# Low parts and two-operand arithmetic from GpSimd to VectorE in a two-layer hybrid diffusion block

## The chip, the cores and the metric

The kernel runs on one core of one Trainium2 chip. A core has five instruction queues that matter here: TensorE (PE in the profile; its weight loads are listed apart, as PEld), VectorE (DVE), ScalarE (ACT), GpSimd (POOL) and SyncE (SP), which issues most DMAs. The metric is the device time of one execution in microseconds; less is better.

## The reference

A backbone of two layers (`DEPTH` = 2) over 256 latent tokens and 256 context tokens of 1024 features. Each layer is:

```
xn = rmsnorm(x) * (1 + scale) + shift            # scale, shift from silu(c) @ w_mod
u  = xn @ w_in                                   # one projection for all three mixers
ya = latent attention, yb = windowed attention with sinks, yc = gated DeltaNet, both directions
y  = (ga*(ya @ w_pa) + gb*(yb @ w_pb) + gc*(yc @ w_pc)) @ w_out
x  = x + gate * y
x  = x + gate * ((silu(a) * b) @ w_down),   a, b = split(dwconv(xn2 @ w_up))
```

Context tokens go through the same weights; in the last layer only what the latent tokens need of them is computed. Inside the DeltaNet, per chunk of 64 tokens and per head:

```
decay = exp(min(gam[i] - gam[j], 0))
a     = strict_lower(k_beta k^T * decay);  qk = lower(q k^T * decay)
u, w  = triangular_solve(a + I, [v*beta, k*beta*exp(gam)])
scan over chunks: v_new = u - w S;  o = q S + qk v_new;  S = S*exp(g_last) + k^T v_new
```

All inputs and outputs are float32. After the two layers a last norm gives the output (1, 256, 1024).

## The kernel before

**Matrix products.** Each float32 operand is taken apart into a high part (rounded to `fp32r`, the type in which TensorE reads it) and a low part (operand minus high part). A product is then three matmuls that add up in one PSUM tile, `mm3` (lines 203 to 206): weight high by activation high (L204), weight high by activation low (L205), weight low by activation high (L206). Two helpers make the parts:

- `load_split` (L186 to 196) loads a piece of weights (`raw`, mostly 128x1024), lets ScalarE cast it to the high part (`wh`, L194) and calls `split_L` (L184) for the low part `wl = raw - wh`.
- `split` (L198 to 200) does the same for activations: cast on ScalarE (L199), difference on VectorE (L200).

`split_L` chooses the engine for `wl` by an accumulator: a fraction `lpool` of the calls goes to GpSimd, the rest to VectorE. The fraction is set per stage: 1.0 for the first modulation, 0 for the projections and the DeltaNet, 0.33 from the attention on and in the feed-forward network (FFN).

**Other work of GpSimd.** GpSimd also does elementwise steps with two SBUF operands: the running sum of squares of a norm (L372); in the DeltaNet's decay `gdn_decay` the gate by a triangle (L809), the decay by the lower mask (L822), beta by a constant (L830) and their product (L834); the scaling by beta in the solve (L921); the state's decay and an addition in the scan (L964, L991); the output norm (L1015); steps of the rotary embedding (L1182, L1237, L1257, L1258, and a copy at L1270); the sum of the merged branches (L1547); and the FFN's product `silu(a) * b` (L1627), whose result goes straight into `split`. Besides, it takes small powers for norms (L348), memsets, masks, some one-operand normalizations of the attention and a few DMAs.

**Stages.** A set-up with the first modulation; per layer the projections and gates, in whose matmuls the DeltaNet's decay, solve and scan are woven (the projections fill TensorE while the DeltaNet's chain waits); attention; merge and `w_out`; and the FFN, two halves of 11 blocks of 128 features, each an up projection and then a down projection. The FFN of the first layer works on 512 columns, that of the last on 256.

**Order.** The instruction streams are fixed when the program is built: a scheduler puts each engine's instructions in order by dependences and priorities (the program can raise the priority of one instruction; such instructions go through a wrapper at L131, so the profile shows them as L131), and each engine then works its queue strictly in that order. In the DeltaNet, `gdn_decay` makes `N` out of the exponential `d`, the products with the keys (`times_k`, L131) and L834; `N` is transposed on VectorE (STREAM_TRANSPOSE, L131), and the solve's matmuls (L845) or the scan's (L957, L971) come in between.

## Time and profile before

| | us |
| --- | --- |
| runs | 1787.89, 1794.27, 1797.77 (median 1794.27) |
| profiled execution: its own time | 1803.63 |
| its span | 1801.8 |
| TensorE busy / idle in the span | 1689.5 / 112.3 |
| VectorE, ScalarE, GpSimd busy | 1082.6, 767.2, 456.0 |

The mean granted TensorE clock of this execution was 0.962. The stages by the timeline: set-up and modulation 0 to 45 us, first projection to 84, DeltaNet of layer 0 with projections to 410, attention to 540, merge and `w_out` to 720, FFN to about 1120; for the last layer projections and DeltaNet to 1410, attention to 1500, merge to 1575, FFN and last norm to the end.

How to read it: busy times are sums over the span, and stages differ much in what they ask of VectorE and GpSimd, so windows of 45 us say more than the sums. A wait is given as "line <- engine and line that ended it". In the timeline a row is one instruction, or several of one line that follow one another (x2, x4), with the engine's wait before it in brackets.

### The profile page before, as it was taken

How to read it: one execution, taken by the hardware profiler on the slowest of the kernel's cores; microseconds unless marked ns; L12 is line 12 of the kernel's file. 1: busy time of each engine (PE TensorE's matmuls, PEld its weight loads, DVE VectorE, ACT ScalarE, POOL GpSimd, SP SyncE). 2: the span in 40 equal slices, each digit the busy share in tenths (PEclk: the TensorE clock that was granted, in tenths of full speed). 3: DMA queues.
4: the chain of work that ended last, by engine and by line, in shares of the span. 5: the costliest groups of instructions: out<-in, count | busy, mean ns of one | idle time of the engine just before them, and what ended most of it. 6: DMA issues, size and time to landing. Idle time of an engine off the chain costs nothing. (4 is left out here: it accounts for less than half of the span.)

```text
span 1801.8 us, 31553 instructions
## 1 busy us (share of the span) xinstructions
PE 1689.5 (94%) x12723; PEld 1371.2 (76%) x12723; DVE 1082.6 (60%) x2089; ACT 767.2 (43%) x1371; POOL 456.0 (25%) x351
## 2 busy tenths in 40 slices
PE   7989888999999999999999999989889899999997
PEld 4768766776557888668888888768777668989996
DVE  2896594565775433445334434798886866466573
ACT  3644411234665233334324333565433564554453
...
GB/s 341 114 80 108 96 88 164 68 85 101 45 117 155 184 136 109 311 170 94 97 103 93 94 155 155 94 88 131 100 100 30 81 59 138 239 122 169 182 171 111
DMA packets 216944, 228.75 MB, mean 127 GB/s; under 512 B 51228, under 2 KB 195422, under 8 KB 215646
## 3 DMA queue, kind: packets, MB, share of 16 engines
...
q8 instruction: 100, 1.64, 0.4%
q14 instruction: 46, 0.38, 0.1%
...
## 5 line engine op out<-in xcount | busy, mean ns | idle before, releaser
L194 ACT CAST wh<-raw 128x1024 fp32r<-128x1024 f32 (+2 forms) x294 | 298.4, 1016 | 412.8 <-PE mm L205 212.8
L184 DVE TENSOR_TENSOR wl<-raw,wh 128x1024 fp32r<-128x1024 f32 (+1 forms) x224 | 280.3, 1252 | 201.9 <-ACT wh L194 182.3
L204 PE MATMUL mm<-xnh,wh 128*128 128x512 f32 (+2 forms) x1072 | 381.6, 357 | 5.6 <-ACT wh L194 2.4
L206 PE MATMUL mm<-xnh,wl 128*128 128x512 f32 (+2 forms) x1072 | 376.1, 353 | 2.6 <-DVE wl L184 1.3
L205 PE MATMUL mm<-xnl,wh 128*128 128x512 f32 (+2 forms) x1072 | 375.5, 351 | 0.7 <-DVE xnl L411 0.6
L184 POOL TENSOR_TENSOR wl<-raw,wh 128x1024 fp32r<-128x1024 f32 (+2 forms) x70 | 162.5, 2322 | 448.7 <-ACT wh L194 419.2
L204 PEld LDWEIGHTS mm<-xnh,wh 128*128 128x128 f32 (+1 forms) x1072 | 206.4, 193 | 39.6 <-issue 7.6
L206 PEld LDWEIGHTS mm<-xnh,wl 128*128 128x128 f32 (+1 forms) x1072 | 205.7, 192 | 33.1 <-issue 2.9
L205 PEld LDWEIGHTS mm<-xnl,wh 128*128 128x128 f32 (+1 forms) x1072 | 206.4, 193 | 28.1 <-DVE xnl L411 2.2
L204 PE MATMUL g<-xnh,wh 128*128 128x256 f32 (+1 forms) x496 | 167.9, 340 | 1.4 <-ACT xnh L410 1.4
L206 PE MATMUL g<-xnh,wl 128*128 128x256 f32 (+1 forms) x496 | 166.6, 337 | 2.1 <-POOL wl L184 2.1
L205 PE MATMUL g<-xnl,wh 128*128 128x256 f32 (+1 forms) x496 | 166.3, 337 | 0.2 <-DVE xnl L411 0.2
L204 PE MATMUL mm<-s,wh 128*128 128x256 f32 (+1 forms) x458 | 151.0, 331 | 2.3 <-ACT s L199 1.7
L206 PE MATMUL mm<-s,wl 128*128 128x256 f32 (+1 forms) x458 | 150.8, 330 | 1.7 <-POOL wl L184 1.1
L205 PE MATMUL mm<-s,wh 128*128 128x256 f32 (+1 forms) x458 | 150.5, 329 | 0.1
L204 PEld LDWEIGHTS g<-xnh,wh 128*128 128x128 f32 x496 | 94.7, 192 | 15.4 <-issue 3.7
L205 PE MATMUL g<-s,wh 128*128 128x512 f32 (+1 forms) x304 | 103.6, 341 | 2.4 <-DVE s L200 2.4
L204 PE MATMUL g<-s,wh 128*128 128x512 f32 (+1 forms) x304 | 104.1, 342 | 1.3 <-ACT s L199 1.3
L206 PEld LDWEIGHTS g<-xnh,wl 128*128 128x128 f32 x496 | 94.6, 191 | 13.2 <-POOL wl L184 2.9
L206 PE MATMUL g<-s,wl 128*128 128x512 f32 (+1 forms) x304 | 103.3, 340 | 0.0
L205 PEld LDWEIGHTS g<-xnl,wh 128*128 128x128 f32 x496 | 94.8, 192 | 10.0 <-DVE xnl L411 0.8
L1627 POOL TENSOR_TENSOR b<-b,b 128x512 f32<-128x512 f32 (+1 forms) x44 | 54.6, 1240 | 170.9 <-DVE b L1611 149.6
...
## 6 DMA issues: line engine op xcount, KB each, us to landing
...
```

The costliest lines, as they stand in the source:

```text
L184: e.tensor_tensor(out=out, in0=x, in1=h.bitcast(F32), op=ALU.subtract)
L194: nc.scalar.copy(H, raw)
L204: mm(ps, lhsT=wH, rhs=xH, start=start, stop=False)
L205: mm(ps, lhsT=wH, rhs=xL, start=False, stop=False)
L206: mm(ps, lhsT=wL, rhs=xH, start=False, stop=stop)
L1627: nc.gpsimd.tensor_tensor(out=y[:, cs], in0=y[:, cs], in1=av[t][:, cs], op=ALU.mult)
```

## The change

`split_L` loses the accumulator and always uses VectorE. Every GpSimd instruction named above that has two operands, and the copy at L1270, is issued on VectorE in its place. The stage fractions (`lpool`, `lp0`, `lpg`, `lpn`, `lpb`) go away. GpSimd keeps the powers of L348, the memsets, the masks, the one-operand normalizations and its DMAs. What is computed stays the same. The queue of GpSimd goes from 294 instructions to 39, that of VectorE from 1981 rows to 2262 (a row can stand for several instructions). The lines shift by 5 to 15: L184 is L179 in the new kernel, L200 L195, L809 L803, L815 L809, L822 L816, L825 L819, L834 L828, L961 L955, L1378 L1372, L1609 and L1611 L1598 and L1600, L1627 L1616.

```diff
@@ -176,12 +176,7 @@
-        self.lacc += self.lpool
-        e = self.nc.vector
-        if self.lacc >= 1.0:
-            self.lacc -= 1.0
-            e = self.nc.gpsimd
-        e.tensor_tensor(out=out, in0=x, in1=h.bitcast(F32), op=ALU.subtract)
+        self.nc.vector.tensor_tensor(out=out, in0=x, in1=h.bitcast(F32), op=ALU.subtract)
...
@@ -369,7 +364,7 @@
-        (e or nc.gpsimd).tensor_tensor(out=self.acc[:, cs], in0=self.acc[:, cs], in1=sq[:, cs], op=ALU.add)
+        (e or nc.vector).tensor_tensor(out=self.acc[:, cs], in0=self.acc[:, cs], in1=sq[:, cs], op=ALU.add)
...
@@ -806,7 +800,7 @@
-                nc.gpsimd.tensor_tensor(out=rg[:, ph], in0=gt["g"][:, s, ph, tl, :].unsqueeze(2).to_broadcast([128, 8, 64]),
+                nc.vector.tensor_tensor(out=rg[:, ph], in0=gt["g"][:, s, ph, tl, :].unsqueeze(2).to_broadcast([128, 8, 64]),
...
@@ -819,7 +813,7 @@
-                    nc.gpsimd.tensor_tensor(out=qk[:, tl, ph], in0=Eq[:, ph],
+                    nc.vector.tensor_tensor(out=qk[:, tl, ph], in0=Eq[:, ph],
...
@@ -827,11 +821,11 @@
-                nc.gpsimd.tensor_tensor(out=bm[:, ph], in0=gt["be"][:, s, ph, tl, :].unsqueeze(2).to_broadcast([128, 8, 64]),
+                nc.vector.tensor_tensor(out=bm[:, ph], in0=gt["be"][:, s, ph, tl, :].unsqueeze(2).to_broadcast([128, 8, 64]),
-            nc.gpsimd.tensor_tensor(out=N[:, tl], in0=d, in1=bm, op=ALU.mult)
+            nc.vector.tensor_tensor(out=N[:, tl], in0=d, in1=bm, op=ALU.mult)
...
@@ -918,7 +912,7 @@
-            nc.gpsimd.tensor_tensor(out=XT[hs, tl, ph], in0=XT[hs, tl, ph],
+            nc.vector.tensor_tensor(out=XT[hs, tl, ph], in0=XT[hs, tl, ph],
...
@@ -961,7 +955,7 @@
-                    nc.gpsimd.tensor_tensor(out=Sn, in0=St, in1=gt["egl"][:, s, ph, tl].unsqueeze(3).to_broadcast([128, 2, 4, 64]), op=ALU.mult)
+                    nc.vector.tensor_tensor(out=Sn, in0=St, in1=gt["egl"][:, s, ph, tl].unsqueeze(3).to_broadcast([128, 2, 4, 64]), op=ALU.mult)
...
@@ -1012,7 +1006,7 @@
-            nc.gpsimd.tensor_tensor(out=hd(oacc[:, tl, :]), in0=hd(oacc[:, tl, :]), in1=r[:, tl, :].unsqueeze(2).to_broadcast([128, 8, 64]), op=ALU.mult)
+            nc.vector.tensor_tensor(out=hd(oacc[:, tl, :]), in0=hd(oacc[:, tl, :]), in1=r[:, tl, :].unsqueeze(2).to_broadcast([128, 8, 64]), op=ALU.mult)
...
@@ -1234,7 +1228,7 @@
-            nc.gpsimd.tensor_tensor(out=t1, in0=xq[:, lat], in1=self.con("cmla"), op=ALU.mult)
+            nc.vector.tensor_tensor(out=t1, in0=xq[:, lat], in1=self.con("cmla"), op=ALU.mult)
...
@@ -1254,8 +1248,8 @@
-            nc.gpsimd.tensor_tensor(out=x, in0=x, in1=self.con("cswa"), op=ALU.mult)
-            nc.gpsimd.tensor_tensor(out=x, in0=x, in1=t2, op=ALU.add)
+            nc.vector.tensor_tensor(out=x, in0=x, in1=self.con("cswa"), op=ALU.mult)
+            nc.vector.tensor_tensor(out=x, in0=x, in1=t2, op=ALU.add)
...
@@ -1624,7 +1613,7 @@
-                    nc.gpsimd.tensor_tensor(out=y[:, cs], in0=y[:, cs], in1=av[t][:, cs], op=ALU.mult)
+                    nc.vector.tensor_tensor(out=y[:, cs], in0=y[:, cs], in1=av[t][:, cs], op=ALU.mult)
...
```

The lines left out are the parameters, the places that set `lpool`, and the same exchange of engine at L408 (which issues nothing with these parameters), L991, L1182, L1270 and L1547.

No priority is changed, but the scheduler places the queues anew. Three places show what that does.

**First place: the second decay of the last layer.** VectorE's queue between the decay and the scan, before. The first operand `s_1898` is `d`, `s_1880` the masked decay `qk`, `s_1879` is `N`, `s_1923` its transpose, and L961 gives the operand for which TensorE's L971 waits.

```order
L131 TENSOR_TENSOR s_1898_11316<-s_1898_11316,g_11372 128x8x64
L131 TENSOR_TENSOR s_1898_11316<-s_1898_11316,g_11382 128x8x64
L184 TENSOR_TENSOR wl_11521<-raw_11518,wh_11520 128x1024
L131 STREAM_TRANSPOSE s_1923_11505<-s_1879_11225 128x1024
L131 TENSOR_TENSOR s_1880_11226<-s_1880_11226,g_11448 128x8x64
L131 TENSOR_TENSOR s_1880_11226<-s_1880_11226,g_11458 128x8x64
L131 TENSOR_TENSOR s_1880_11226<-s_1880_11226,g_11468 128x8x64
L131 TENSOR_TENSOR s_1880_11226<-s_1880_11226,g_11478 128x8x64
L131 STREAM_TRANSPOSE s_1923_11505<-s_1879_11225 32x1024 x2
L961 TENSOR_TENSOR b_1930_11536<-g_11488,gtb_10178 128x512
```

The same place after:

```order
L179 TENSOR_TENSOR wl_11521<-raw_11518,wh_11520 128x1024
L816 TENSOR_TENSOR s_1880_11226<-s_1901_11323,cst 128x512 x2
L131 TENSOR_TENSOR s_1898_11316<-s_1898_11316,g_11372 128x8x64
L131 TENSOR_TENSOR s_1898_11316<-s_1898_11316,g_11382 128x8x64
L131 TENSOR_TENSOR s_1880_11226<-s_1880_11226,g_11448 128x8x64
L828 TENSOR_TENSOR s_1879_11225<-s_1898_11316,s_1902_11331 128x1024
L131 TENSOR_TENSOR s_1880_11226<-s_1880_11226,g_11458 128x8x64
L131 TENSOR_TENSOR s_1880_11226<-s_1880_11226,g_11468 128x8x64
L131 TENSOR_TENSOR s_1880_11226<-s_1880_11226,g_11478 128x8x64
L131 STREAM_TRANSPOSE s_1923_11505<-s_1879_11225 128x1024
L955 TENSOR_TENSOR b_1930_11536<-g_11488,gtb_10178 128x512
L131 STREAM_TRANSPOSE s_1923_11505<-s_1879_11225 32x1024 x2
```

The three products that GpSimd made (L816 twice, L828) now stand in VectorE's queue, and L961 (L955 after) is put ahead of the two transposes of 32 partitions instead of behind them.

**Second place: the second decay of layer 0.** VectorE's queue before; `s_142` and `s_282` are the two masked decays that the products with queries fill, `s_325` is the transpose of `N` (`s_281`).

```order
L131 STREAM_TRANSPOSE s_325_2121<-s_281_1854 128x1024
L131 TENSOR_TENSOR s_142_769<-s_142_769,g_2008 128x8x64
L131 TENSOR_TENSOR s_142_769<-s_142_769,g_2018 128x8x64
L131 TENSOR_TENSOR s_142_769<-s_142_769,g_2028 128x8x64
L131 TENSOR_TENSOR s_142_769<-s_142_769,g_2038 128x8x64
L131 TENSOR_TENSOR s_282_1855<-s_282_1855,g_2048 128x8x64
L131 TENSOR_TENSOR s_282_1855<-s_282_1855,g_2058 128x8x64
L131 TENSOR_TENSOR s_282_1855<-s_282_1855,g_2068 128x8x64
L131 TENSOR_TENSOR s_282_1855<-s_282_1855,g_2078 128x8x64
L131 STREAM_TRANSPOSE s_325_2121<-s_281_1854 32x1024 x2
L961 TENSOR_TENSOR b_327_2150<-g_2089,gtb_754 128x512
```

After:

```order
L131 TENSOR_TENSOR s_142_769<-s_142_769,g_2028 128x8x64
L131 TENSOR_TENSOR s_142_769<-s_142_769,g_2038 128x8x64
L131 TENSOR_TENSOR s_282_1855<-s_282_1855,g_2048 128x8x64
L131 TENSOR_TENSOR s_282_1855<-s_282_1855,g_2058 128x8x64
L131 TENSOR_TENSOR s_282_1855<-s_282_1855,g_2068 128x8x64
L131 TENSOR_TENSOR s_282_1855<-s_282_1855,g_2078 128x8x64
L131 TENSOR_TENSOR s_297_1927<-s_297_1927,g_1963 128x8x64
L131 TENSOR_TENSOR s_297_1927<-s_297_1927,g_1973 128x8x64
L955 TENSOR_TENSOR b_327_2150<-g_2089,gtb_754 128x512
L828 TENSOR_TENSOR s_281_1854<-s_297_1927,s_301_1942 128x1024
L179 TENSOR_TENSOR wl_2236<-raw_2233,wh_2235 128x1024
L131 STREAM_TRANSPOSE s_325_2121<-s_281_1854 128x1024
```

The eight products stood behind the first transpose and now stand ahead of it; the product that makes `N` (L828) stands between them and the transpose. At the same place ScalarE's queue changes as well, before (L820 and L827 are the decay's exponentials, L1378 a sigmoid of the merge gates):

```order
L820 ACT_TABLE_LOAD
L820 ACTIVATE s_287_1866<-s_287_1866 128x1024
L827 ACTIVATE s_284_1859<-s_284_1859 128x1024
L194 CAST wh_2175<-raw_2173 128x1024
L820 ACTIVATE s_300_1934<-s_300_1934 128x1024
L827 ACTIVATE s_297_1927<-s_297_1927 128x1024
L1378 ACT_TABLE_LOAD
L1378 ACTIVATE b_307_1990<-mm_1898 128x512
```

and after:

```order
L814 ACT_TABLE_LOAD
L814 ACTIVATE s_287_1866<-s_287_1866 128x1024
L821 ACTIVATE s_284_1859<-s_284_1859 128x1024
L189 CAST wh_2175<-raw_2173 128x1024
L1372 ACT_TABLE_LOAD
L1372 ACTIVATE b_307_1990<-mm_1898 128x512
L814 ACT_TABLE_LOAD
L814 ACTIVATE s_300_1934<-s_300_1934 128x1024
L1373 DMA gates_262<-b_307_1990 128x512
L1372 ACT_TABLE_LOAD
L1372 ACTIVATE b_308_2005<-mm_1899 128x512
L821 ACT_TABLE_LOAD
```

The exponentials no longer stand side by side but between the sigmoids, with a table load at each change; over the whole program ScalarE has 44 table loads in place of 38.

**Third place: the up projection in the last layer's FFN.** VectorE's queue before; L1609 and L1611 are the convolution, `b_2583` the block that the next step splits at L200:

```order
L184 TENSOR_TENSOR wl_15324<-raw_15321,wh_15323 128x1024
L1609 SCALAR_TENSOR_TENSOR b_2583_15263<-mm_15213,fcv_91,b_2583_15263 128x255
L1611 SCALAR_TENSOR_TENSOR b_2583_15263<-mm_15213,fcv_91,b_2583_15263 128x255
L184 TENSOR_TENSOR wl_15366<-raw_15363,wh_15365 128x1024
L200 TENSOR_TENSOR s_2541_14989<-b_2583_15263,s_2537_14985 128x256
L1609 SCALAR_TENSOR_TENSOR b_2584_15282<-mm_15214,fcv_91,b_2584_15282 128x255
L1611 SCALAR_TENSOR_TENSOR b_2584_15282<-mm_15214,fcv_91,b_2584_15282 128x255
L200 TENSOR_TENSOR s_2541_14989<-b_2584_15282,s_2537_14985 128x256
```

GpSimd's queue at the same place before:

```order
L1627 TENSOR_TENSOR b_2564_15134<-b_2564_15134,b_2554_15060 128x256
L184 TENSOR_TENSOR wl_15294<-raw_15291,wh_15293 128x1024
L1627 TENSOR_TENSOR b_2583_15263<-b_2583_15263,b_2573_15191 128x256
L1627 TENSOR_TENSOR b_2584_15282<-b_2584_15282,b_2574_15208 128x256
L184 TENSOR_TENSOR wl_15396<-raw_15393,wh_15395 128x1024
L1627 TENSOR_TENSOR b_2603_15411<-b_2603_15411,b_2593_15339 128x256
```

and VectorE's after, which holds both:

```order
L179 TENSOR_TENSOR wl_15324<-raw_15321,wh_15323 128x1024
L1598 SCALAR_TENSOR_TENSOR b_2583_15263<-mm_15213,fcv_91,b_2583_15263 128x255
L1600 SCALAR_TENSOR_TENSOR b_2583_15263<-mm_15213,fcv_91,b_2583_15263 128x255
L1616 TENSOR_TENSOR b_2583_15263<-b_2583_15263,b_2573_15191 128x256
L179 TENSOR_TENSOR wl_15366<-raw_15363,wh_15365 128x1024
L195 TENSOR_TENSOR s_2541_14989<-b_2583_15263,s_2537_14985 128x256
L1598 SCALAR_TENSOR_TENSOR b_2584_15282<-mm_15214,fcv_91,b_2584_15282 128x255
L1600 SCALAR_TENSOR_TENSOR b_2584_15282<-mm_15214,fcv_91,b_2584_15282 128x255
L1616 TENSOR_TENSOR b_2584_15282<-b_2584_15282,b_2574_15208 128x256
L179 TENSOR_TENSOR wl_15396<-raw_15393,wh_15395 128x1024
L195 TENSOR_TENSOR s_2541_14989<-b_2584_15282,s_2537_14985 128x256
```

The FFN's products (L1616) stand between the convolution and the split, and a weight's low part that was GpSimd's stands between a product and its split.

## Rows read from the trace of the kernel before

**Rows 1.** The page's first part: busy time, share and instructions of each engine.

```profile
PE 1689.5 (94%) x12723; PEld 1371.2 (76%) x12723; DVE 1082.6 (60%) x2089; ACT 767.2 (43%) x1371; POOL 456.0 (25%) x351
```

**Rows 2.** TensorE's waits, whole span: waiting line <- releaser: us, times, longest.

```profile
PE g L971 <- DVE b L961: 9.6, 4, 7.4
...
PE g L845 <- DVE s L131: 4.3, 1, 4.3
...
PE g L694 <- ACT s L677: 3.5, 1, 3.5
...
PE g L1020 <- POOL s L1015: 2.6, 4, 1.3
PE g L1254 <- DVE b L1256: 2.5, 1, 2.5
PE g L205 <- DVE s L200: 2.4, 2, 1.8
...
PE mm L206 <- POOL wl L184: 2.3, 3, 1.1
...
PE g L206 <- POOL wl L184: 2.1, 3, 0.8
```

**Rows 3.** Groups by shape on GpSimd: count | busy us, mean ns | idle before.

```profile
L184 POOL TENSOR_TENSOR wl<-raw,wh 128x1024 fp32r<-128x1024 f32 x64 | 153.6, 2399 | 397.5 <-ACT wh L194 368.0 <-DVE s L1566 13.3 <-PE g L206 11.8
```

**Rows 4.** The same view of VectorE: low parts of weights and of activations.

```profile
L184 DVE TENSOR_TENSOR wl<-raw,wh 128x1024 fp32r<-128x1024 f32 x200 | 258.5, 1293 | 195.1 <-ACT wh L194 175.6 <-issue 16.9 <-POOL wl L184 2.3
...
L200 DVE TENSOR_TENSOR s<-b,s 128x256 fp32r<-128x256 f32 x22 | 25.0, 1135 | 24.0 <-ACT s L199 24.0
...
L200 DVE TENSOR_TENSOR s<-s,s 128x256 fp32r<-128x256 f32 x20 | 8.0, 420 | 12.7 <-ACT s L199 12.7
```

**Rows 5.** The same view of ScalarE: the table loads of the decay's exponential.

```profile
L820 ACT ACT_TABLE_LOAD x3 | 3.8, 1283 | 1.2 <-ACT b L1378 1.2
```

**Rows 6.** Timeline, last layer's second decay: start, duration (us), engine, [wait].

```profile
1268.23 3.18 DVE L184 TENSOR_TENSOR wl<-raw,wh 128x1024 fp32r<-128x1024 f32 x1
...
1275.58 1.29 DVE L131 TENSOR_TENSOR s<-s,g 128x512 f32<-128x512 f32 x2 [1.13 <-ACT s L827]
...
1276.79 1.22 DVE L184 TENSOR_TENSOR wl<-raw,wh 128x1024 fp32r<-128x1024 f32 x1
...
1277.04 3.22 POOL L834 TENSOR_TENSOR s<-s,s 128x1024 f32<-128x1024 f32 x1 [0.57 <-DVE s L131]
...
1280.29 2.01 DVE L131 STREAM_TRANSPOSE s<-s 128x1024 f32<-128x1024 f32 x1 [2.29 <-POOL s L834]
...
1284.67 3.80 DVE L131 STREAM_TRANSPOSE s<-s 32x1024 f32<-32x1024 f32 x2
1288.50 0.69 DVE L961 TENSOR_TENSOR b<-g,gtb 128x512 f32<-128x512 f32 x1
```

**Rows 7.** Timeline, last layer's attention preparation, VectorE.

```profile
1413.28 3.34 DVE L1244 TENSOR_TENSOR s<-b,b 32x256 f32<-32x256 f32 x3
```

**Rows 8.** Timeline, last layer's up projection, GpSimd and VectorE.

```profile
1597.30 2.39 POOL L184 TENSOR_TENSOR wl<-raw,wh 128x1024 fp32r<-128x1024 f32 x1
...
1597.82 2.16 DVE L200 TENSOR_TENSOR s<-b,s 128x256 fp32r<-128x256 f32 x1 [0.25 <-ACT s L199]
```

**Rows 9.** Windows: stretch, us; busy (count) of each engine; PEclk; DMA share; GB/s.

```profile
90.00:135.00 45.00, 39.38 (x190) 31.22 (x189) 40.97 (x91) 22.27 (x44) 15.29 (x13) 0.92 0.28 79
224.00:229.00 5.00, 4.66 (x82) 4.47 (x83) 4.99 (x9) 0.00 (x0) 0.00 (x0) 0.53 0.00 0
1170.00:1215.00 45.00, 39.89 (x251) 31.16 (x250) 41.16 (x87) 27.66 (x52) 16.45 (x14) 0.96 0.31 88
1289.00:1294.00 5.00, 4.75 (x48) 4.50 (x50) 5.00 (x11) 0.38 (x1) 2.03 (x1) 0.54 0.41 84
1395.00:1440.00 45.00, 38.69 (x193) 29.07 (x193) 37.87 (x94) 25.05 (x54) 18.86 (x20) 0.85 0.29 83
1600.00:1646.00 46.00, 44.62 (x367) 43.97 (x367) 31.34 (x46) 25.32 (x44) 21.40 (x12) 1.00 0.56 172
```

More of the change, by code (lines that the diff above doesn't have):

```diff
@@ L89 @@
     l1={}, s2=(2, 1, 2, 0), pe=(0.0, 0.1, 0.0, 0.0), ov=0, np=(0.1, 0.0, 0.25, 0), ly=2, qs=(0, 4), dec1=3.0, dec2=4.0, sol1=4.2, sol2=4.0,
-    sol3=1.0, sol4=2.0, sca=(1.0, 2.0), scb=(1.0, 2.0), scc=(1.0, 2.0), lpg=0.0, lpn=0.33, cap=12.0, sl=(0.3, 0.3, 0.5, 0.1), modc=(4.0, 0.9),
+    sol3=1.0, sol4=2.0, sca=(1.0, 2.0), scb=(1.0, 2.0), scc=(1.0, 2.0),   cap=12.0, sl=(0.3, 0.3, 0.5, 0.1), modc=(4.0, 0.9),
     lag=(0, 0, 2, 4, 5), nmod=(2, 5), hk=(5, 12), f0=(1.0, 1.6, 1.0, 1.0, 1.5, 1.0, 1.0), f1=(1.0, 1.0, 1.0, 0.3, 1.0, 1.0, 0.3), lat=1.0,
     bx=4, wd=0, dc=1, gk=(0, 0), hpe=60, w_t=5, w_k=3, w_s=0, w_r=1.5, w_n=3, w_o=4.0, nr=3, nh=3, nl=4, nb2=7, st=0, ab=(0.0, 0.0, 0.0, 0.0),
-    st2=6, lp0=1.0, lpb=0.33, bge=2, hpa=40, hpn=0, hpk=40, hpv=40)
+    st2=6, bge=2, hpa=40, hpn=0, hpk=40, hpv=40)
 _INS = ["x", "c", "ctx", "c_ctx", "w_mod", "b_mod", "norm1", "norm2", "w_in", "mla_q_norm", "mla_kv_norm",
@@ L407, in norm_mod @@
                 self.pri(nc.scalar, "hpn").copy(XH[k][:, c], t)
-                nc.gpsimd.tensor_tensor(out=XL[k][:, c], in0=t, in1=XH[k][:, c].bitcast(F32), op=ALU.subtract)
+                nc.vector.tensor_tensor(out=XL[k][:, c], in0=t, in1=XH[k][:, c].bitcast(F32), op=ALU.subtract)
                 continue
@@ L438, in setup @@
             self.AB.append(self.per.tile([128, 2, KD, 2], F32, name=f"AB{l}"))
-        self.lpool = self.P["lp0"]
         m = self.m0 = self.modulation_first()
@@ L990, in gdn_scan @@
                     if n >= 2:
-                        nc.gpsimd.tensor_tensor(out=t, in0=t, in1=o3, op=ALU.add)
+                        nc.vector.tensor_tensor(out=t, in0=t, in1=o3, op=ALU.add)
                     self.pri(nc.vector, "hps").tensor_tensor(out=o3, in0=t, in1=pqk, op=ALU.add)
@@ L1181, in mla_kv @@
         t1, t2 = self.b2([128, S]), self.b2([128, S])
-        nc.gpsimd.tensor_tensor(out=t1[32:64], in0=m[:, lat], in1=self.con("cmla")[32:64], op=ALU.mult)
+        nc.vector.tensor_tensor(out=t1[32:64], in0=m[:, lat], in1=self.con("cmla")[32:64], op=ALU.mult)
         nc.vector.tensor_tensor(out=t2[32:64], in0=pr[32:64, :S], in1=self.con("smla")[32:64], op=ALU.mult)
@@ L1269, in swa_prep @@
             nc.scalar.copy(kk[a, g], sk[a])
-            nc.gpsimd.tensor_copy(kk[b, g], kk[a, g].bitcast(F32))
+            nc.vector.tensor_copy(kk[b, g], kk[a, g].bitcast(F32))
             nc.vector.tensor_tensor(out=kl[a], in0=sk[a], in1=kk[a, g].bitcast(F32), op=ALU.subtract)
@@ L1406, in layer @@
         self.mark(f"gproj_{l}")
-        if l:
-            self.lpool = self.P["lpg"]
         self.gdn_alloc()
@@ L1420, in layer @@
         self.queue = [gq, gv, gkv, self.gates]
-        self.lpool = self.P["lpg"]
         spill = self.dram.tile([128, KD, T], F32, name=f"spill{l}")
@@ L1457, in layer @@
         finish(gsq, gmq)
-        self.lpool = self.P["lpn"]
         yc = A["zs"]
@@ L1546, in ev @@
                         nc.vector.tensor_tensor(out=sg[t], in0=p[:, cs], in1=sg[t], op=ALU.mult)
-                        nc.gpsimd.tensor_tensor(out=mt, in0=mt, in1=sg[t], op=ALU.add)
+                        nc.vector.tensor_tensor(out=mt, in0=mt, in1=sg[t], op=ALU.add)
                 self.run_gen(self.linear(i["w_branch_" + b][l], 0, 4, u * 256, 256, yy, ev, cols=lambda _: slice(0, n)))
@@ L1580, in norm2 @@
             yield from self.norm_mod(xT, self.AB[l][:, 1], self.mod[l][:, 3], *self.X2, s)
-        self.lpool = self.P["lpb"]
         self.run_gen(self.linear(i["w_out"][l], 0, KD, 0, D, (mH, mL), residual(2, 0, True), cols=lambda _: slice(0, n),
@@ L1635, in layer @@
                                          split=0 if f == 0 and not last else None, hook=lambda: norm2(1)))
-                self.lpool = self.P["lpn"]
                 self.run_gen(self.linear(i["ffn_up"][l], 0, KD, (f + 22) * 128, nf * 128, X, evb, cols=c_o))
@@ L1639, in layer @@
                 self.final_load()
-            self.lpool = self.P["lpb"] if half else self.P["lpn"]
             self.run_gen(self.linear(i["ffn_down"][l], f0, 11, 0, D, (aH, aL), residual(5, None, half == 1), cols=c_o,
@@ L1657, in run @@
         self.NRAW, self.NWH, self.NWL, self.NMM = self.P["nr"], self.P["nh"], self.P["nl"], 3
-        self.lpool, self.lacc = 0.0, 0.0
         self.queue, self.bg, self.gcount, self.bg_every, self.credit, self.modcost, self.gates, self.wait, self.sq_last, self.bgx, self.unit, self.wide = [], [], 0, 3, 0.0, 4.0, None, 0.0, None, None, 0, False
```

## The prediction

> **What bounds the kernel now.** I read first the page's busy shares, then TensorE's waits, then windows of 45 us with the groups by shape, and last the timeline where a wait had a neighbour on GpSimd. TensorE is busy 1689.5 of 1801.8 us (94%), so all that can be won are its 112.3 idle us and what its clock loses; VectorE has 60% and GpSimd 25% [rows 1]. No TensorE instruction is added or taken away, so a faster VectorE alone gives nothing: an edit counts where TensorE waits for VectorE or GpSimd. These waits are spread over many places of a few us each [rows 2], and the reader is to see there that the longest (7.4 us at L971, 4.3 at L845) name VectorE, while those that name GpSimd are short.
>
> Most of what GpSimd does is hidden. But it costs in a second way, which the groups show: one shape of VectorE's instruction has two durations. The difference for a 128x256 activation takes 420 ns in one set of 20 and 1135 in another of 22 [rows 4]. In the timeline such a one of 2.16 us starts 0.5 us after a GpSimd instruction of 2.39 us and ends just after it [rows 8]: VectorE stood still until GpSimd was done. The low parts of weights show it too, 1293 ns on the average and 1.22 where GpSimd is quiet, once 3.18 [rows 4, 6].
>
> **The change part by part.** By its code 299 of GpSimd's 351 instructions [rows 1] go to VectorE: 72 of 1024 elements per partition, 4 of 768, 130 of 512, 93 of 256. On VectorE an instruction took 1.22, 0.69 and 0.42 us for 1024, 512 and 256 [rows 4, 6]; for 768 I take 0.95, between the first two. That is 88 + 4 + 90 + 39 = 221 us more for VectorE, against at most 456 less for GpSimd: half a us of VectorE for one of GpSimd. (A weight's low part goes from 2.40 [rows 3] to 1.22.) VectorE gets back its stalls; two shapes alone hold 200 x (1.293 - 1.21) = 16.6 and 25.0 - 22 x 0.42 = 15.8, together 32.4 us [rows 4]. So VectorE comes to some 1270 us, 70% of the span. Off the critical path both are free.
>
> *Waits that go.* (a) L971, 7.4 us, the last layer's second decay [rows 6]. VectorE waits 2.29 us for GpSimd's L834 (3.22), transposes (2.01), does four products and two transposes of 32 partitions (3.80), and only then L961, at 1288.50. After, L961 stands ahead of the 3.80. I lay the new queue out from the end of the weight's low part at 1278.01, less the 1.29 of the two products that now follow it: 1276.72. Then two masks (2 x 0.69), the two products (1.29), four more (2.58), N (1.22) and the transpose (2.01) make 8.5, to 1285.2. Ahead of that, the other decay's N (1.22) and two constants (1.38) come in, and the stall of the 3.18 (1.97) goes: 1285.8 against 1288.50, **-2.7**. (b) L845, 4.3 us, the same place in layer 0: eight products of 0.645 (5.2 us) stood behind a transpose that waits for GpSimd and stand ahead of it now; I leave 1 us of wait, **-3.3**. (c) L694, 3.5 us: ScalarE's L677 needs a VectorE step that the old queue held behind the transposes of the first decay and the new one puts ahead of them; **-2.5**. (d) L1254, 2.5 us: three rotary products ahead took 3.34 us, and 3 x 0.42 is 1.26 [rows 7]; **-2.0**. (e) TensorE's waits for a low part made by GpSimd, 2.3 + 2.1 us [rows 2]: the part now comes after 1.22 and not 2.40; **-3.4**. (f) L205 behind the slow split, 2.4 us [rows 2, 8]: **-2.0**, since the split falls to 0.42 but has the product (0.42) and a low part (1.22) ahead of it on one engine. (g) L1020 behind L1015, 2.6 us: **-1.0**. Together -16.9. Gone waits leave what was late next: in (a) and (b) the transposes and products, all VectorE.
>
> *Clock.* After the two long waits the granted clock fell, to 0.53 and 0.54 over 5 us [rows 9], that is, about half of that time at 1.2 GHz: 5 x 0.46 = 2.3 us each. (b) nearly goes, so its 2.3 go; of (a) more than half stays, so I take half: **-3.5**. If any long wait keeps the clock low, 0.
>
> *Cost: dense windows.* VectorE is full in the DeltaNet's preparations: 40.97 of 45 us at 90 to 135, 41.16 at 1170 to 1215, 37.87 at 1395 to 1440, with 15.29, 16.45 and 18.86 of GpSimd beside it [rows 9]. Half of the latter moved makes 48.6, 49.4 and 47.3: over by 3.6 + 4.4 + 2.3 = 10.3 us. The trace shows no such overload, so the bounds are far apart. Below: the stalls go too (32.4/456 = 0.07 us per us of GpSimd, 3.6 for these windows), nothing is late, -3.6. Above: all the moved work is on the path, 25.2. I take half of the overflow, **+5**: the fullest window near it, 41 of 45, has TensorE busy over 39 us, and its neighbours have room for some backlog, but not for a chain. In the last FFN the room suffices: 31.34 of 46, and its 12 GpSimd instructions [rows 9] are at most four low parts and eight products, 4 x 1.22 + 8 x 0.42 = 8.2, so 39.5.
>
> The Trainium skill ("Perfetto Trace Analysis", section "Optimizing Scalar/DVE Operations") says that with a saturated VectorE offloading to ScalarE or even GpSimd may make sense, and adds that GpSimd shares an SBUF read port with it, so that it might not help. It speaks against the change in these three windows: by it the sum would take 25.2 there rather than 5. Its second half agrees with the 2.16 us of [rows 8].
>
> *Cost: tables.* Six more table loads of 1.283 us on ScalarE [rows 5], 7.7 in all, at layer 0's decays. ScalarE has 22.27 of 45 us there [rows 9], so most is covered; 0 to 7.7, and I take **+1**. Without that cover each would delay the exponential and all of the decay behind it.
>
> *Sum.* -16.9 - 3.5 + 5 + 1 = -14.4 us. The profiled execution took 1803.63; 1789.2 is the same execution after the change. The median of the runs is 1794.27, 0.9948 of the profiled one: **1780 us**.
>
> **The rivals.** *Eaten* (no change): the windows pay all 10.3, and the gains (a) to (d), 10.5 us, are lost, for they lie in just those stretches; the clock stays. Left are (e) to (g), -6.4, so -6.4 + 10.3 + 1 = +4.9, which gives 1799. For it: (a) and (b) already name VectorE, not GpSimd. Against it: 2.29 us of that chain is a plain wait for GpSimd [rows 6]. *VectorE as the bound* (slower): in the three windows the decay's and gates' chain goes through VectorE alone, and what GpSimd did beside it is put on it end to end: 25.2 - 3.6 + 7.7 for the tables - 6.4 = +22.9, which gives 1817. It decides once TensorE's idle time in these windows (5.6 + 5.1 + 6.3 = 17.0 us now [rows 9]) grows by more than the 20 us that the rest can give. For it: 91% of VectorE. Against it: TensorE's fill-in matmuls are in queue order and need few VectorE steps. *All relief* (faster still): the windows and tables cost nothing, and what (a), (e) and (g) left goes too, the three shorter waits of L971 among it (2.2 + 1.6 + 1.0), with the other half of the clock (1.1): -20.4 - 5.9 = -26.3, which gives 1768. For it: VectorE's half price for the same work, and the stalls; against it: where VectorE is full, no wait has to go.
>
> **How the numbers follow.** 0.5% is 9 us, about what a measurement here can tell from no change: 1785.3 to 1803.2. Chances: forecast 0.50 (its own range 1768 to 1794; 0.38 below 1785.3), eaten 0.22 (0.02 faster, 0.15 same, 0.05 slower), VectorE as the bound 0.13 (0.12 slower), all relief 0.15. Faster 0.55, same 0.28, slower 0.17. Range 1758 to 1804: below it lies a tail of the last case, with another third of the 32.4 us of stalls on the path; above it most of the slower case.
>
> **What would show it.** Right: the 128x256 splits all near 0.42 us and weights' low parts near 1.21; no wait of L206 for GpSimd; L971's wait near 4.7 and L845's near 1; TensorE's idle time near 100 us. Wrong: windows of VectorE above 44 of 45 us with TensorE below 38 in them; new waits of L204 to L206 for VectorE's low parts in the last FFN; ScalarE's exponentials late behind table loads. The step most likely to fail is the +5.

## The result and the profile after

The changed kernel took 1787.74 us (median of 16 runs, 1784.49 to 1800.26), the kernel before 1798.23 (16 runs): a ratio of 0.9942, 95% interval 0.9922 to 0.9962. That is faster, by a little over half a per cent. The profiled execution took 1788.72 us (before: 1803.63), with a span of 1786.9.

The page's first part, to be read against [rows 1]:

```profile
PE 1686.1 (94%) x12723; PEld 1366.2 (76%) x12723; DVE 1213.1 (68%) x2388; ACT 777.6 (44%) x1377; POOL 33.8 (2%) x52
```

TensorE's idle time fell from 112.3 to 100.8 us. VectorE's busy time rose by only 1213.1 - 1082.6 = 130.5 us where 219 moved to it (its new instructions at their durations in this trace). It got back 68 us of stalls: by so much the instructions that it had before became shorter. The other 20 us or so are no gain: neighbouring records overlap by some 0.05 us each, which a sum of durations counts and busy time does not. TensorE's waits (line <- releaser: us, times, longest), against [rows 2]:

```profile
PE g L1094 <- DVE b L1084: 10.4, 3, 7.8
...
PE g L951 <- DVE b L940: 7.9, 5, 4.9
PE mm L201 <- DVE wl L179: 7.9, 4, 3.5
PE g L877 <- DVE s L131: 6.3, 1, 6.3
...
PE g L965 <- DVE b L955: 3.7, 3, 2.1
PE g L935 <- DVE b L968: 3.3, 1, 3.3
...
PE g L1248 <- DVE b L1250: 1.9, 1, 1.9
...
PE g L839 <- DVE s L131: 0.2, 1, 0.2
```

L839 is L845 of before (4.3 us, now 0.2), L965 is L971 (9.6, now 3.7), L1248 is L1254 (2.5, now 1.9); the waits for GpSimd's L1015 and low parts are gone, L694's too. New ones have come, all for VectorE: L1094 in the attention (7.8 in one piece), L877 in the solve (6.3; before, as L883, 3.6), L951 and L935 in the scan, and L201 for weights' low parts that VectorE makes (7.9; before, as L206, 1.9): 3.5 and 1.0 at 121 and 129 us in layer 0, 3.2 at 1183 in the last layer. VectorE's groups (count | busy us, mean ns), against [rows 4]:

```profile
L179 DVE TENSOR_TENSOR wl<-raw,wh 128x1024 fp32r<-128x1024 f32 x264 | 322.5, 1222 | 238.4 <-ACT wh L189 237.7
...
L195 DVE TENSOR_TENSOR s<-b,s 128x256 fp32r<-128x256 f32 x22 | 9.2, 418 | 0.0
...
L195 DVE TENSOR_TENSOR s<-s,s 128x256 fp32r<-128x256 f32 x20 | 7.6, 416 | 0.2 <-PE g L200 0.2
```

All are at their undisturbed durations: 1.22 us, and 0.42 where the mean was 1.135. The three dense windows, against [rows 9]:

```profile
90.00:135.00 45.00, 40.46 (x224) 31.11 (x221) 40.37 (x87) 26.97 (x45) 1.04 (x2) 0.96 0.25 71
1170.00:1215.00 45.00, 39.30 (x254) 32.63 (x251) 42.21 (x82) 25.21 (x45) 1.03 (x2) 0.92 0.32 94
1395.00:1440.00 45.00, 33.32 (x141) 21.70 (x141) 38.63 (x104) 25.90 (x56) 2.43 (x2) 0.80 0.11 27
```

VectorE is hardly fuller than before (40.97, 41.16 and 37.87): the forecast's overflow did not come about. TensorE's idle time in them is 4.5, 5.7 and 11.7 us; before it was 5.6, 5.1 and 6.3.

**Where the time went.** The two traces are laid side by side at points that both pass on TensorE: the ends of the DeltaNet's output (L1020) and of the attentions' last product (L1116) in each layer, and the norms' L391. Durations in us, each of one profiled execution; the other kernels are those of the next section.

| kernel | A: to the end of layer 0's DeltaNet | B: its attention | C: merge and FFN | D: last layer's projections, DeltaNet | E: its attention | F: merge | G: FFN, end | span |
| --- | --- | --- | --- | --- | --- | --- | --- | --- |
| before | 402.6 | 165.2 | 555.0 | 283.9 | 96.5 | 77.1 | 221.5 | 1801.8 |
| changed | 386.4 | 171.4 | 554.4 | 289.5 | 104.6 | 75.1 | 205.4 | 1786.9 |
| ffn1 | 403.4 | 165.2 | 554.8 | 286.3 | 93.9 | 76.2 | 205.4 | 1785.2 |
| ffn1_prod | 404.7 | 165.2 | 555.1 | 283.7 | 96.5 | 77.3 | 206.7 | 1789.1 |
| low | 403.5 | 164.9 | 553.9 | 283.5 | 90.9 | 75.0 | 205.4 | 1777.2 |
| gdn | 388.0 | 169.9 | 555.5 | 291.8 | 96.3 | 76.7 | 221.7 | 1799.8 |
| low_gdn0 | 386.8 | 170.1 | 554.5 | 281.6 | 92.2 | 74.5 | 206.7 | 1766.4 |
| low_gdn1 | 398.2 | 162.8 | 554.7 | 293.1 | 97.6 | 75.0 | 206.2 | 1787.6 |
| low_att | 399.5 | 171.0 | 554.6 | 280.5 | 101.4 | 75.0 | 205.9 | 1787.9 |
| attn_back | 387.7 | 161.1 | 554.5 | 296.3 | 94.6 | 75.1 | 205.5 | 1774.8 |
| best2 | 387.9 | 168.1 | 554.6 | 286.8 | 93.2 | 74.6 | 206.1 | 1771.2 |
| dup2 | 383.5 | 167.4 | 554.9 | 293.1 | 104.8 | 75.1 | 217.7 | 1796.4 |
| dup1 | 387.7 | 165.6 | 554.3 | 292.8 | 104.7 | 75.1 | 205.5 | 1785.9 |

The last two are the changed kernel up to stage G, so their A to F show how far one execution strays: by 4 to 6 us in A, B and D, by 0.2 in E and F. The change gained in A (-16.2) and G (-16.1), lost in B (+6.2), D (+5.6; 9 in the other two executions) and E (+8.1), and F and C gave 2.6.

Part of this is not waiting: TensorE's busy time for the same matmuls changed too, and with it the granted clock. Busy us (granted clock) in windows cut at whole us near those points:

| kernel | A | B | C | D | E | F | G |
| --- | --- | --- | --- | --- | --- | --- | --- |
| before | 364.5 (0.94) | 156.0 (0.95) | 550.6 (1.00) | 254.2 (0.94) | 88.2 (0.93) | 73.4 (0.98) | 202.7 (0.95) |
| changed | 358.6 (0.97) | 159.6 (0.90) | 551.3 (1.00) | 258.7 (0.92) | 89.8 (0.90) | 72.7 (0.99) | 195.5 (0.97) |

The clock gave 5.9 us in A and 7.2 in G, and took 3.6 in B, 4.5 in D and 1.6 in E. The rest of each difference is idle time: 10 us less in A, 9 less in G, 6.5 more in E, but only 1 more in D.

### The profile page after: what moved, and what is told of

Read it like the earlier page. It is cut to its first block, busy times and chain, and to the rows that moved or that the text cites. A ratio compares the mean times of both kernels' runs of the same rounds, so it can differ in the third digit from the quotient of the medians.

```text
span 1786.9 us, 31353 instructions
## 1 busy us (share of the span) xinstructions
PE 1686.1 (94%) x12723; PEld 1366.2 (76%) x12723; DVE 1213.1 (68%) x2388; ACT 777.6 (44%) x1377; POOL 33.8 (2%) x52
## 5 line engine op out<-in xcount | busy, mean ns | idle before, releaser
L179 DVE TENSOR_TENSOR wl<-raw,wh 128x1024 fp32r<-128x1024 f32 (+2 forms) x294 | 348.0, 1184 | 242.9 <-ACT wh L189 242.0
L201 PE MATMUL mm<-xnh,wl 128*128 128x512 f32 (+2 forms) x1072 | 375.4, 352 | 7.9 <-DVE wl L179 7.9
L200 PE MATMUL mm<-xnl,wh 128*128 128x512 f32 (+2 forms) x1072 | 375.5, 351 | 0.2
L199 PEld LDWEIGHTS mm<-xnh,wh 128*128 128x128 f32 (+1 forms) x1072 | 205.5, 192 | 40.7 <-issue 8.6
L201 PEld LDWEIGHTS mm<-xnh,wl 128*128 128x128 f32 (+1 forms) x1072 | 205.7, 192 | 39.1 <-DVE wl L179 10.1
L200 PEld LDWEIGHTS mm<-xnl,wh 128*128 128x128 f32 (+1 forms) x1072 | 205.5, 192 | 28.2 <-issue 4.4
L200 PE MATMUL g<-xnl,wh 128*128 128x256 f32 (+1 forms) x496 | 166.4, 337 | 0.2 <-DVE xnl L406 0.2
L201 PE MATMUL g<-xnh,wl 128*128 128x256 f32 (+1 forms) x496 | 166.1, 336 | 0.0
L201 PE MATMUL mm<-s,wl 128*128 128x256 f32 (+1 forms) x458 | 150.9, 330 | 0.0
L200 PE MATMUL mm<-s,wh 128*128 128x256 f32 (+1 forms) x458 | 150.3, 329 | 0.0
L199 PEld LDWEIGHTS g<-xnh,wh 128*128 128x128 f32 x496 | 94.6, 192 | 15.0 <-issue 2.5
L201 PEld LDWEIGHTS g<-xnh,wl 128*128 128x128 f32 x496 | 94.6, 191 | 10.6 <-issue 0.8
L200 PEld LDWEIGHTS g<-xnl,wh 128*128 128x128 f32 x496 | 94.7, 191 | 10.0 <-DVE xnl L406 0.8
L200 PE MATMUL g<-s,wh 128*128 128x512 f32 (+1 forms) x304 | 102.2, 336 | 0.0
L201 PE MATMUL g<-s,wl 128*128 128x512 f32 (+1 forms) x304 | 102.2, 336 | 0.0
L199 PEld LDWEIGHTS mm<-s,wh 128*128 128x128 f32 x458 | 87.9, 193 | 8.4 <-DVE s L534 0.9
L201 PEld LDWEIGHTS mm<-s,wl 128*128 128x128 f32 x458 | 88.7, 194 | 7.0
```

Source lines behind the costliest of these rows:

```text
L179: self.nc.vector.tensor_tensor(out=out, in0=x, in1=h.bitcast(F32), op=ALU.subtract)
L199: mm(ps, lhsT=wH, rhs=xH, start=start, stop=False)
L200: mm(ps, lhsT=wH, rhs=xL, start=False, stop=False)
L201: mm(ps, lhsT=wL, rhs=xH, start=False, stop=stop)
```

## The experiments

**Theories.** The forecast's: many short waits go (A to G), and a little is lost where VectorE is full. Its rivals: the stages differ in sign, so that two large gains are half eaten by VectorE as the bound in the last layer; or the gain is one stage's alone. Eleven kernels, each timed against the kernel before, whose median in these comparisons was 1799.8 to 1801.5 us; between kernels the ratios compare better than the microseconds.

**ffn1**, only the last FFN:

```diff
@@ evb; before the second half of ffn_up; before ffn_down
-nc.gpsimd.tensor_tensor(out=y[:, cs], ...)
+(nc.vector if last else nc.gpsimd).tensor_tensor(out=y[:, cs], ...)
-self.lpool = self.P["lpn"]
+self.lpool = 0.0 if last else self.P["lpn"]
```

> The kernel before, with only the last layer's FFN changed: its products (L1627) and all its weights' low parts (L184) on VectorE; TensorE's queue is that of before, row for row. Theory A (the forecast's terms e and f: waits for a GpSimd-made low part and one slow split): about -5 us against before, ratio 0.997, and TensorE's idle time in the last 220 us falls from some 15 to 10. Theory B (the whole of what the two traces show there, 14.5 us between 1577 us and the end, is GpSimd's doing in this stage): -14 us, ratio 0.992, as much as the whole change gave. Rival C (it was the earlier stages that handed this one a better start): no change, within 2 us.

Measured: 1782.19 us, 0.9901 (0.9877 to 0.9925): theory B. Stage G went from 221.5 to 205.4, as in the changed kernel, with TensorE's queue untouched. This stage alone gives more than the whole change.

**low**, all weights' low parts and nothing else (`lp0`, `lpn`, `lpb` = 0; `lpg` was 0 already):

> The kernel before, with only the low parts of all weights (L184) on VectorE; GpSimd keeps all its arithmetic. Theory A (forecast, term e): -3.4 us, ratio 0.998. Theory B (64 instructions of 2.4 us on GpSimd stall VectorE, and most of the 14.5 us in the last FFN are theirs): -8 us or more, ratio 0.9955 or less. Rival C: the low parts queue on VectorE behind the DeltaNet's work and the kernel is slower by 2 us or more.

Measured: 1778.54 us, 0.9878 (0.9854 to 0.9902): theory B, and more: 9 us better than the changed kernel. G is 205.4 though the FFN's products stay on GpSimd; E and F gain 5.6 and 2.1 (in E the scheduler also placed TensorE's queue anew).

**ffn1_prod**, only the products of the last FFN (the first pair of lines of ffn1's diff):

> The kernel before with only the products of the last FFN (L1627, 22 instructions of 256 elements) on VectorE; a third of the weights' low parts stays on GpSimd; TensorE's queue is that of before. Theory A (the low parts on GpSimd make the loss, late and by stalling VectorE): within 3 us of before, ratio 0.998 to 1.002, with L206 still waiting for GpSimd. Theory B (the chain product, cast, split through GpSimd is the loss): half or more of the 16 us, ratio 0.9955 or less.

Measured: 1785.07 us, 0.9908 (0.9877 to 0.9938): theory A falls, and B's amount comes without B's reason, since in **low** the products were left where they were and G was the same. Moving either of the two is enough: what costs is both of them on GpSimd. The stall of VectorE alone, **low**'s theory B, does not make the loss: in ffn1_prod the slow split still takes 917 ns on the mean, against 415 in **low**, and the gain is there all the same. The timeline of before (start, duration, engine, [wait]) around the low part of [rows 8]:

```profile
1595.63 1.04 ACT L194 CAST wh<-raw 128x1024 fp32r<-128x1024 f32 x1
...
1596.61 0.73 POOL L1627 TENSOR_TENSOR b<-b,b 128x256 f32<-128x256 f32 x1 [17.59 <-DVE b L1611]
...
1599.74 0.39 PE L206 MATMUL g<-xnh,wl 128*128 128x256 f32 x1 [0.68 <-POOL wl L184]
```

The cast that the low part needs is done at 1596.67, but on GpSimd a product stands ahead of it, which waited for the convolution; the low part starts at 1597.30 and TensorE waits 0.68 us for it. Four of L206's five waits over 0.6 us in this stage are of this kind; in the fifth (0.61 at 1645) the low part starts at once and its own 2.39 us are too long. The same place in ffn1_prod:

```profile
1597.66 1.04 ACT L194 CAST wh<-raw 128x1024 fp32r<-128x1024 f32 x1
...
1598.77 2.44 POOL L184 TENSOR_TENSOR wl<-raw,wh 128x1024 fp32r<-128x1024 f32 x1 [17.65 <-ACT wh L194]
```

Here it starts 0.07 us after the cast, takes its 2.44 us, and of L206's waits for GpSimd one of 0.2 us is left in the stage. The rest is the clock. Windows of before (stretch, length, busy of PE, PEld, DVE, ACT, POOL, then PEclk):

```profile
1660.00:1665.00 5.00, 4.52 (x25) 4.32 (x26) 2.72 (x4) 2.13 (x3) 2.39 (x1) 0.72 0.33 105
1665.00:1670.00 5.00, 5.00 (x42) 5.00 (x41) 1.23 (x1) 1.41 (x2) 0.00 (x0) 0.93 0.56 186
1760.00:1765.00 5.00, 3.23 (x15) 3.03 (x16) 3.72 (x4) 1.16 (x2) 1.66 (x1) 0.62 0.67 215
1765.00:1770.00 5.00, 5.00 (x32) 5.00 (x32) 2.04 (x4) 1.81 (x6) 0.00 (x0) 0.69 0.55 176
```

They follow waits of 1.7 us (L204 for ScalarE's cast behind a late product) and of 1.3 + 1.8 us (L204 again, then L205 for a split that takes 2.12 us beside a low part on GpSimd: here the stall does have a part). 5 x (0.28 + 0.07 + 0.38 + 0.31) = 5.2 us is an estimate of what went to the lower clock of 1.2 GHz in them, a little high because TensorE was idle for part of the time; in ffn1_prod the same stretches show 1.00. The whole stage tells it better: TensorE's busy time fell by 7.2 us in the changed kernel. The waits of stage G that are gone (five for L206, 3.9 us, three of 4.7 in all where the up projection's two halves end) and these 7.2 make 15.8 of its 16.1.

**dup2 and dup1**, the changed kernel with GpSimd work that nobody reads:

```diff
@@ evb, ahead of the split; o is the half of y that the last layer leaves unused
+if last:
+    for _ in range(4):
+        nc.gpsimd.tensor_tensor(out=y[:, o], in0=y[:, cs], in1=av[t][:, cs], op=ALU.mult)   # dup2
+        nc.gpsimd.tensor_scalar(out=y[:, o], in0=y[:, cs], scalar1=fc[:, 0:1], ...)         # dup1
```

> The changed kernel; in the last FFN GpSimd makes each of the 22 products four times more, with two SBUF operands and 256 elements, into an unused half of the block's buffer, and nobody reads them. Queues of the other engines stay as they are. Theory A (two-operand GpSimd work stalls VectorE even if nobody waits for its result): the 128x256 splits rise from 0.42 us to 0.7 or more, VectorE's busy time between the last norm and the end rises by 10 us or more, and the kernel loses 2 to 8 us against the changed one. Theory B (GpSimd cost only because its results were waited for): splits at 0.42 to 0.5 and no change within 2 us.

> As the run with the doubled products, but GpSimd's 88 added instructions have one SBUF operand and a per-partition scalar (the form of its normalizations in the attention). Theory A (the stall needs two SBUF operands on GpSimd): splits at 0.42 to 0.5 us and no change against the changed kernel within 2 us. Theory B (any GpSimd instruction that reads SBUF stalls VectorE's two-operand ones): splits at 0.7 us or more, as with two operands.

Measured: dup2 1802.17 us, 1.0012 (0.9993 to 1.0032); dup1 1787.48 us, 0.9932 (0.9906 to 0.9959). Theory A in both, and dup2's price (+14 us by the medians, +12.3 in stage G) is above its range. GpSimd's and VectorE's groups in dup2:

```profile
L1631 POOL TENSOR_TENSOR b<-b,b 128x256 f32<-128x256 f32 x88 | 97.1, 1108 | 86.3 <-DVE b L1627 60.0 <-ACT b L1606 20.7 <-issue 0.4
```
```profile
L200 DVE TENSOR_TENSOR s<-b,s 128x256 fp32r<-128x256 f32 x22 | 20.7, 940 | 0.0
```

and in dup1:

```profile
L1631 POOL TENSOR_SCALAR b<-b,fcv 128x256 f32<-128x256 f32 x88 | 115.0, 1311 | 59.7 <-DVE b L1627 33.2 <-ACT b L1606 20.4
```
```profile
L200 DVE TENSOR_TENSOR s<-b,s 128x256 fp32r<-128x256 f32 x22 | 9.1, 414 | 0.0
```

With two operands 97 us of GpSimd raise the split from 418 to 940 ns; with one operand 115 us leave it at 414. So the stall is real without any dependence, and nearly all of it needs GpSimd's second operand: VectorE's busy time in stage G is 148.5 us in the changed kernel, 171.9 in dup2 and 152.5 in dup1 (there its products go from 425 to 513 ns, its low parts from 1224 to 1262). The price in dup2 reaches TensorE in four waits of 1.1 to 1.2 us for the cast and the split where the halves of the up projection end, and in the clock: TensorE is busy 202.2 us in the stage against 195.0. The Trainium skill ("Perfetto Trace Analysis", section "Optimizing Scalar/DVE Operations") has the two engines share an SBUF read port. dup2 agrees; dup1 shows that a GpSimd instruction that reads SBUF need not cost VectorE much, 4 us for 115.

**gdn**, only the DeltaNet's eight lines on VectorE in both layers:

> The kernel before, with only the DeltaNet's eight GpSimd lines (L809 to L1015) on VectorE. Theory A (forecast, terms a to c and g, the clock and the dense windows): about -8 us, ratio 0.9955, with L845's wait gone and L971's at 2 to 5 us. Theory B (layer 0 gains 20 us as the traces show, and the last layer's second half and the attention behind it give 7 to 14 back): between -5 and -13, with the two long waits gone and a new wait of 5 us or more of the last layer's solve or scan for VectorE. Rival C (VectorE full in the dense windows, GpSimd's help missed): slower than before by 5 us or more.

Measured: 1801.14 us, 1.0000 (0.9980 to 1.0019), outside the ranges of theories A and B, and not theory C. The table tells why: stage A gains 14.6 (theory B had 20), D loses 7.9, with L883's wait at 6.8 us and L957's at 4.9 as theory B had it, and stage B loses 4.7 more. **low_gdn0** and **low_gdn1** take the layers apart:

```diff
@@ layer(), before the DeltaNet
+self.gv = nc.gpsimd if l else nc.vector      # low_gdn0; the other way round in low_gdn1
@@ L809, L822, L830, L834, L921, L964, L991, L1015
-nc.gpsimd.tensor_tensor(...)
+self.gv.tensor_tensor(...)
```

> All low parts on VectorE, and the DeltaNet's eight lines on VectorE in layer 0 alone; all else of GpSimd stays. Theory A (the two layers differ: in the traces so far layer 0 gained 15 us from the moved DeltaNet up to its end and the last layer lost 6 to 8, so that the run with both showed nothing): 10 to 15 us better than low parts alone, ratio to before 0.980 to 0.983. Theory B (layer 0's gain is spent again in its own attention, since the fill-in matmuls are used up earlier): within 4 us of low parts alone, ratio 0.986 to 0.990. Rival C (VectorE's added work costs in layer 0 as well): ratio 0.991 or more.

> All low parts on VectorE, and the DeltaNet's eight lines on VectorE in the last layer alone. Theory A (in the last layer, whose projections have half the columns, VectorE's chain of the decay and the solve is the bound and the moved work lengthens it): 5 to 10 us slower than low parts alone, ratio to before 0.990 to 0.994, with a wait of TensorE for the solve's VectorE steps (L883) of over 5 us. Theory B (the loss there came from arriving earlier out of layer 0): within 2 us of low parts alone, ratio 0.987 to 0.989.

Measured: low_gdn0 1770.10 us, 0.9836 (0.9809 to 0.9863); low_gdn1 1792.59 us, 0.9951 (0.9932 to 0.9971). The first falls between theory A (0.980 to 0.983) and theory B (0.986 to 0.990), with both in the table: stage A gains 16.7 against low, and stage B gives 5.2 back. The second is theory A and beyond: +14 us against low by the medians, and 9.6 in stage D of the traces. Of these 9.6 only 2.4 are idle time; 7.1 are TensorE's busy time (253.7 us in low, 260.8 here), and the granted clock is lower where the longer waits are (0.86 against 1.00 from 1180 to 1200 us, 0.78 against 0.96 from 1320 to 1340). TensorE's waits of low_gdn1:

```profile
PE g L957 <- DVE b L946: 9.8, 7, 4.9
PE g L883 <- DVE s L131: 6.4, 1, 6.4
```

The solve is a chain of VectorE steps, and in the last layer, where the projections have 256 columns, TensorE has no fill-in work left before the chain is done. That the number of columns is the reason is a reading of the traces; no run changed it. In the changed kernel (timeline):

```profile
1326.96 3.62 PE L877 MATMUL g<-s,s 32*32 32x32 f32 x128 [6.35 <-DVE s L131]
...
1340.47 0.48 PE L951 MATMUL g<-b,s 64*64 64x64 f32 x4 [4.89 <-DVE b L940]
```

**attn_back** and **low_att** test the rotary products and the copy (L1182, L1237, L1257, L1258, L1270): the changed kernel with these back on GpSimd, and low with these on VectorE.

> The changed kernel, with the rotary products and the copy before the attention (L1182, L1237, L1257, L1258, L1270) back on GpSimd. Theory A (the 7 us that each attention lost in the changed kernel's trace come from these moved instructions on VectorE): -10 to -14 us against the changed kernel, ratio to before about 0.987. Theory B (they come from the projections' fill-in matmuls having been used up earlier in the queue, so that TensorE stands bare in the attention): no more than 3 us from the changed kernel, ratio 0.993 to 0.996, with L1094 still waiting for VectorE for over 5 us in one piece.

> All low parts on VectorE, and the rotary products and the copy before the attention (L1182, L1237, L1257, L1258, L1270) too; the DeltaNet stays on GpSimd. Theory A (these products on VectorE cost 11 us whatever else is moved): ratio to before 0.993 to 0.995. Theory B (they cost only together with the moved DeltaNet, by the clock that TensorE gets in the attention: 0.61 over 20 us in the changed kernel, 0.83 without them): within 3 us of low parts alone, ratio 0.986 to 0.990.

Measured: attn_back 1779.55 us, 0.9880 (0.9852 to 0.9908), 8 us better than the changed kernel by the medians, a little short of theory A's 10 to 14; low_att 1793.94 us, 0.9973 (0.9952 to 0.9994), 15 us worse than low: theory A, and above its range. TensorE's waits in low_att over the whole span (the 7.8 us are in stage E), and the same wait in the changed kernel's timeline:

```profile
PE g L1100 <- DVE b L1090: 10.7, 4, 7.8
...
PE g L1100 <- DVE sm L131: 9.3, 7, 2.9
```

```profile
1430.62 0.69 DVE L1265 TENSOR_TENSOR s<-s,s 64x512 fp32r<-64x512 f32 x1
...
1432.76 1.74 DVE L1282 TENSOR_TENSOR s<-s,s 64x256 fp32r<-64x256 f32 x4
...
1434.73 1.69 DVE L1282 TENSOR_TENSOR s<-s,s 64x256 fp32r<-64x256 f32 x3
1434.86 1.73 POOL L1084 TENSOR_SCALAR b<-b,sm 128x512 f32<-128x512 f32 x1 [36.20 <-DVE sm L131]
1436.43 0.88 DVE L1084 TENSOR_SCALAR b<-b,sm 128x512 f32<-128x512 f32 x2
...
1437.06 1.09 PE L1094 MATMUL g<-cst,b 128*128 128x128 f32 x4 [7.78 <-DVE b L1084]
```

The softmax's normalization (L1084) stands in VectorE's queue behind the splits of the windowed queries (L1265, L1282), and TensorE waits 7.78 us. In low and attn_back no such wait is over 1.6 us in this stage. In the kernel before, too, such splits stand ahead of the normalization, but TensorE has 4.3 us of projection matmuls there (L204 to L206, 1435.67 to 1439.96) and then waits 1.27 us; in the changed kernel such matmuls come only behind the wait. How much of it is VectorE's order and how much these matmuls was not taken apart. Stage B lost 6.2 us, but there the clock plays in, from 480 to 500 us of the changed kernel and of attn_back:

```profile
480.00:500.00 20.00, 17.69 (x88) 8.84 (x80) 10.64 (x38) 10.54 (x33) 0.00 (x0) 0.61 0.59 184
```
```profile
480.00:500.00 20.00, 16.71 (x91) 10.38 (x91) 13.89 (x47) 14.04 (x41) 0.00 (x0) 0.83 0.52 157
```

A PEclk of 0.61 against 0.83 is 4.4 us in 20, and runs with the same instructions up to there differ by 6 us; stage B is left open.

**best2**, low_gdn0 with the sums of squares (L372), the merge's sum (L1547) and the FFN's products on VectorE too:

> All low parts, the sums of squares, the merge's sum and the FFN's products on VectorE, and the DeltaNet's lines in layer 0 alone; the rotary products and the last layer's DeltaNet stay on GpSimd. Theory A (layer 0 as in the run with the attention's products back, 19 us better at its merge, and the last layer as with low parts and layer 0's DeltaNet): -40 us, ratio 0.976 to 0.980. Theory B (the sums and products off the path give nothing more): ratio 0.982 to 0.985, as without them.

Measured: 1774.27 us, 0.9845 (0.9817 to 0.9873): theory B; theory A rested on attn_back's short stage B, and that did not repeat (168.1 against 161.1). **The best version is low_gdn0**, 0.9836, with best2 inside its interval: low parts and layer 0's DeltaNet on VectorE, the last layer's DeltaNet and the rotary products on GpSimd.

## Why the forecast came out, and which of its steps did not

The number held: 1780 forecast, 1787.7 measured, 1789.2 against 1788.72 for the profiled execution. That the last two agree so closely is luck: single executions of the kernel before lie between 1787.9 and 1805.6. By the medians of 16 runs the change gave 10.5 us, not 14.4, and the 1780 rested on a median of three runs (1794.27) that became 1798.23 with sixteen. The sum behind the number held only in total; its terms were off by up to 13 us, in both signs, and cancelled.

- *TensorE bounds, only its waits and its clock count*: right. Its idle time fell by 11.5 us, its busy time by 3.4. That the latter meets the forecast's clock term of 3.5 is luck as well: it is 13.1 us given in A and G, and most of it taken again in B, D and E. And a granted clock of 0.53 over 5 us is nearly all of that time at 1.2 GHz, not half of it; the price of 2.3 us is right.
- *VectorE to 1270 us*: 1213; the stalls were worth 68 us, not 32. They were priced from two shapes, and others had them: the 128x512 splits (L200) went from 911 to 687 ns on the mean, and the one-operand L825 from 902 to 481. The rest is the overlap of neighbouring records.
- *(a) L971, -2.7*: 7.4 us became 0.9 + 3.3 (L965 and L935), -3.2. The two transposes that L961 passed now delay the scan's next step.
- *(b), (c) and their clock, -8.1*: the waits went as said (0.2 and none left), but the decay's transposes, which had held them up, now hold up a weight's low part, and TensorE waits 3.5 + 1.0 us for it (lines below). Stage A still gained 16.2, and 14.6 to 16.7 in gdn and low_gdn0: 10 of it idle time, with L845's other wait (2.1) and L1020's gone, and 5.9 the clock. The mechanism is right at half its size; a few us of the stage were not traced.
- *(d) L1254, -2.0*: 2.5 became 1.9, so most of it stayed. *(g) L1020, -1.0*: 2.6 became less than 0.2.
- *(e), (f), -5.4*: the step that was mis-sized most on this side. Stage G gained 16.1. I took the low part's own 2.40 us for the delay; it was mostly the product ahead of it in GpSimd's queue (four of the five waits), and moving either away cured it, as **low** and **ffn1_prod** show. Short waits there also cost some 7 us by the clock, which I gave only to the two long waits of the DeltaNet.
- *Dense windows, +5*: the step that failed on the other side. I looked for overload in windows and halved it; there was none (VectorE 40.4, 42.2 and 38.6 of 45 us), and it is chains that pay. D lost 5.6 and E 8.1 although (a) gained 3.2 and (d) 0.6 in them: a price of 17.5 us, within the upper bound of 25.2. Of D's loss 4.5 are the clock after longer waits. Layer 0 pays too, at 90 to 135 us:

```profile
115.97 3.95 DVE L131 STREAM_TRANSPOSE s<-s 32x1024 f32<-32x1024 f32 x2
...
120.04 1.22 DVE L179 TENSOR_TENSOR wl<-raw,wh 128x1024 fp32r<-128x1024 f32 x1
...
121.31 0.50 PE L201 MATMUL mm<-xnh,wl 128*128 128x512 f32 x1 [3.48 <-DVE wl L179]
```

  Each run with layer 0's DeltaNet on VectorE has this wait, and each run with the last layer's one of 3.2 us at the same place there. The forecast had looked for waits on low parts in the last FFN, where none came. The rival of VectorE as the bound was thus right in the last layer's two stretches; in layer 0 the gains were larger than the price. What kept it from deciding were A and G.
- *The Trainium skill's rule.* By "Perfetto Trace Analysis", section "Optimizing Scalar/DVE Operations", a saturated VectorE may be worth offloading even to GpSimd. D and E agree in sign: leaving the work on GpSimd is worth 9.6 us in D (low against low_gdn1) and 10.0 to 10.5 in E (attn_back against the changed kernel, low against low_att). But VectorE was busy in only 81% of D and 70% of E before the change, and no run here shows that saturation is what decides.
- *Tables, +1*: no cost seen; stage A, which holds the six added loads, gained most.
